# Per-tile norm factors, transposed halves of dt and one power for the last rows in a gMLP and Mamba-2 block on one core

## The chip, the cores and the metric

The kernel runs on one core of a Trainium2 chip. The metric is the device time of one execution in microseconds. Five engines work side by side, each through its own list of instructions in order: PE (TensorE, products and transposes), DVE (VectorE), ACT (ScalarE), POOL (GpSimd) and SP (SyncE, which issues most loads). ACT issues the stores. The profile shows each instruction with its source line, its tiles, and what ended the idle time ahead of it.

## The reference

One layer on a sequence of 1024 rows and 1024 columns, all in float32: an adaptive norm whose scale and shift come from a conditioning vector, one wide projection, a gated spatial branch, a state-space branch, two projections back, and a final norm. What the change touches:

```python
def rms_norm(x, w):
    xf = x.astype(jnp.float32)
    y = xf * lax.rsqrt(jnp.mean(xf * xf, axis=-1, keepdims=True) + EPS)
    return (y * w.astype(jnp.float32)).astype(x.dtype)

mod = jax.nn.silu(c) @ ada_w + ada_b
shift, scale, gate = jnp.split(mod, 3, axis=-1)
h = rms_norm(x, norm_w) * (1 + scale[:, None, :]) + shift[:, None, :]
proj = h @ w_in
...
dt = jax.nn.softplus((dt_raw + dt_bias).astype(jnp.float32))
...
x = x + gate[:, None, :] * (merged @ w_out)
return rms_norm(x, final_norm_w)
```

The norm of `h` needs one factor for each row, the power -1/2 of its mean square; dt_raw is 32 columns of the projection; the last line needs such a factor again.

## The kernel before

**Products.** Each large product is done with seven half-size products of the Strassen-Winograd kind (p1 to p7), and each float32 operand is split into a high and a low part (`hi`, `lo`, names that end in h and l), so that a product is three passes over four 128x512 pieces (L591). A bank in PSUM is emptied by a copy or an addition (L728, results such as c1g, c2g, c2z, c2x: letters for columns group, numbers for the halves of rows). p4 of a group adds onto a bank that the addition into c2 must have read before, so PE waits for that VectorE instruction.

**Head.** Eight tiles of x (128 rows each, `xt`, x_238 to x_245 in the lists below) are loaded. `square` (L376, ACT) gives a tile's sums of squares, `factors` (L380 on VectorE, L381 on GpSimd) the factors of four tiles at once, `normed` scales half a tile (left columns are half 0). Then PE transposes pieces of the scaled tiles (L94, px), a matrix-vector product `matvec` (L91, pm<-aw,scz) and `modulation` give scale and shift (md), and `rows_of_h` writes the transposed h and its parts (hf, b11h, b11l; b12 for tiles 4 to 7). The first weights are split in `split_w0` (w0l, w0d). Products with ones and the identity (`warm`, acc<-ones,ident) fill PE between. All of the head is written with `pin`: its order on each engine is that of the code. After the first product passes the loop calls `prepare(1)`, which makes the second half.

**Middle.** Beside the projection run three sorts of side work, spread over the products by `later(n, f)`, which puts f behind n more products: the quarters of the second projection's weights (`wb_quarter` and what follows it, tiles wbr, wba, wbb, wbc, stored to wb_d), the gate's weights (`gated_weights`, tile wog, stored to wo_d), and dt. The projection has left dt as two halves of 32 rows (one for the high and one for the low part of the operands) in dt_d, 64 rows by 1024. `dt_part1` loads them (dtt), `dt_part1a` brings them into rows by chunk and adds the two halves: eight products with `fold`, two identity pieces on top of one another, into the bank pdtt, with the bias added as the bank is read (L806). Steps with the tile sm (L807 to L836) compute softplus from it. What is not pinned here is ordered on VectorE and ScalarE by a scheduler that works from its own costs, so one more instruction can move many others.

**Tail.** The last product leaves rows in banks; `after_bank` adds them to the rows' tile r, squares, takes the factor with one power on GpSimd (`roots_of`, L1958 and L1959) and scales (L2007, L2008). The last row tile is done in two pieces of 256 columns (L2049 to L2057); its factor is computed by `last_root`, three Newton steps on VectorE from an integer estimate (L1964 to L1968).

```python
    mm(pt[:, ch * NH : (ch + 1) * NH], dtt[:, ch * P : (ch + 1) * P], fold[0][0 : 2 * NH, :])
V.tensor_tensor(v3(dtr), v3(pt[:, 0:n]), bc(dtb), op=ALU.add)
...
last_root(3)
V.tensor_scalar_mul(rows[3][:, LEFT], rows[3][:, LEFT], root[:, 3:4])
```

Of the kernel before, what the change touches and what calls it, by code (L numbers as in the profile page):

```python
# [16 lines left out]
P = 128  # L17
# [6 lines left out]
NH = 32  # L24
# [11 lines left out]
def hybrid_kernel(  # L36
# [106 lines left out]

    hpool = tc.tile_pool(name="hpool", bufs=1, reuse_waits="tile")
    hp = hpool.__enter__()
    BANKS = (1, 2, 0, 4, 5, 6, 3, 7)
    BN = ("b11", "t1", "t2", "b22", "t3", "b21", "t4")
    bop = {}
    for nm in BN:
# [30 lines left out]
    with tc.tile_pool(name="p0", bufs=1, reuse_waits="tile") as p0:  # L180
# [72 lines left out]
        def warm(n):  # L253

            for _ in range(n):
                mm(accs[2][1][:, 0:P], ident, ones)
# [118 lines left out]
        def square(t):  # L375
            pin(A.activation(junk, xt[t], AF.Square, accum_out=sq0[:, t : t + 1]))  # L376

        def factors(b):
            bs = slice(4 * b, 4 * b + 4)
            pin(V.tensor_scalar(sq0[:, bs], sq0[:, bs], 1.0 / D, EPS, op0=ALU.mult, op1=ALU.add))  # L380
            pin(G.tensor_tensor(rs[:, bs], sq0[:, bs], nhalf[:, bs], op=ALU.pow))  # L381

# [6 lines left out]

        for t in range(4):  # L390
            square(t)
        factors(0)
        for t in range(4):
            normed(t, 0, V)
        transposes(0, 0)
        split_w0(0)
        for t in range(4):
            normed(t, 1, V)
        matvec(0)
        warm(3)  # L400
        modulation(0)
        warm(8)
        rows_of_h(0, 0)
        for t in range(4, NCH):
            square(t)
        factors(1)
        for half in range(2):
            for t in range(4, NCH):
                normed(t, half, A if t > 5 else V)
        split_w0(1)  # L410

        def prepare(n):

            if n == 1:
                return {
                    8: lambda: (warm(6), transposes(0, 1), rows_of_h(0, 1), matvec(1), warm(5)),
                    11: lambda: (transposes(1, 1), modulation(1), rows_of_h(1, 1)),
                    16: lambda: (transposes(1, 0), rows_of_h(1, 0)),
                }
            a, b = halves(n)  # L420
            return {
                2: lambda: (matvec(n), transposes(n, a)),
                6: lambda: (modulation(n), rows_of_h(n, a)),
                14: lambda: (transposes(n, b), rows_of_h(n, b)),
            }
# [360 lines left out]
    def dt_part1():  # L786

        dtt = wide("dtt2")[0 : 2 * NH, :]
        load(dtt, dt_d)
        load(dtb, dt_bias.to_broadcast([P, NH]))  # L790
        load(abc, a_log.to_broadcast([P, NH]))
        V.tensor_add(fold[0], ident[:, 0:NH], ident[:, NH : 2 * NH])
        sm1 = wide("sm1").rearrange("p (a n) -> p a n", a=4)
        sm2 = wide("sm2").rearrange("p (a n) -> p a n", a=4)
        later(2, dt_part1a, dtt, sm1, sm2)

    def dt_part1a(dtt, sm1, sm2):
        v3 = lambda t: t.rearrange("p (a b) -> p a b", a=NCH)
        bc = lambda t: t.unsqueeze(1).to_broadcast([P, NCH, NH])
        n = NCH * NH  # L800
        e, q, pl, dtr = (sm1[:, i] for i in range(4))
        dth, adt = sm2[:, 0], sm2[:, 1]
        pt = bank("pdtt")
        for ch in range(NCH):
            mm(pt[:, ch * NH : (ch + 1) * NH], dtt[:, ch * P : (ch + 1) * P], fold[0][0 : 2 * NH, :])
        V.tensor_tensor(v3(dtr), v3(pt[:, 0:n]), bc(dtb), op=ALU.add)  # L806
        V.scalar_tensor_tensor(e, dtr, -1.0, dtr, op0=ALU.mult, op1=ALU.max)  # L807
        A.activation(e, e, AF.Exp, scale=-1.0)
        later(2, dt_part1b, e, q, pl, dtr, dth, adt)
# [616 lines left out]
        return done  # L1426

    todo = jobs + tail
    fold = []
    NPRE = 19  # L1430
    pre = None
    ops = pair_weights(*todo[0][:3], pinned=True)
# [4 lines left out]
    for n, (name, _, _, d1, d2, g) in enumerate(todo):  # L1437
        if n == 3:
            later(1, mix_load, 0)
        if n == NPRE:  # L1440
            gate_kept()
            gxpool.__exit__(None, None, None)
            prepool = tc.tile_pool(name="prepool", bufs=1, side="right", reuse_waits="tile")
            pre = prepool.__enter__()

            fold.append(pre.tile([P, NH], F32, name="fold", tag="fold"))
            wb_load(0)
            for i in range(len(quarters)):
                later(2 + 4 * i, wb_quarter, i)
# [388 lines left out]
    ps3 = tc.tile_pool(name="ps3", bufs=1, space=PSUM, reuse_waits="tile")  # L1838
    psb = ps3.__enter__()
    numbered(psb, "q")  # L1840
    places_of = {"x": (3, 1, 0, 2), "y": range(4, 8)}
    assert all(b > 3 for b in free[6:])
    OB = {"p1": 0, "p5": 1, "p7": 2, "p4": 3, "p6": 4, "p2": 5, "p3": 6}
    OORDER = ("p1", "p5", "p6", "p7", "p4", "p3", "p2")
# [113 lines left out]
        V.scalar_tensor_tensor(var[:, ts], sql[:, ts], 1.0 / D, sqr[:, ts], op0=ALU.mult, op1=ALU.add)  # L1958
        G.tensor_tensor(root[:, ts], var[:, ts], nhalf[:, ts], op=ALU.pow)  # L1959

    def last_root(t):

        y, t, v = root[:, 3:4], sql[:, 4:5], sql[:, 5:6]
        V.tensor_scalar(y.bitcast(I32), var[:, 3:4].bitcast(I32), -0.5, float(0x5F3759DF), op0=ALU.mult, op1=ALU.add)  # L1964
        V.tensor_scalar_mul(v, var[:, 3:4], -0.5)
        for _ in range(3):
            V.scalar_tensor_tensor(t, y, y, v, op0=ALU.mult, op1=ALU.mult)
            V.scalar_tensor_tensor(y, t, 1.5, y, op0=ALU.add, op1=ALU.mult)  # L1968

    def multiplied(ps, nm, j, cs, w):  # L1970
        a, first = mop[OUT[nm][1]], nm in ("p1", "p5", "p2")
        for k in range(4):
# [67 lines left out]
    for nm in OORDER:  # L2040
        ps, m = out_banks[OUT[nm][0]], OUT[nm][1]
        if nm == "p2":
            variance(slice(0, 4))
        for j in range(4):
            if nm == "p2" and j == 3:
                pieces = ((ps[3][:, 0:256], slice(0, 256)), (banks_last[:, 0:256], slice(256, 512)))
                for n, (acc, cs) in enumerate(pieces):
                    multiplied(acc, nm, 3, cs, 256)
                    V.tensor_add(rows[3][:, cs], rows[3][:, cs], acc)  # L2049
                    square(3, cs, sql[:, 3 + 4 * n : 4 + 4 * n])  # L2050
                    G.tensor_mul(rows[3][:, cs], rows[3][:, cs], fnw[:, cs])
                    V.scalar_tensor_tensor((sqr if n == 0 else var)[:, 3:4], sql[:, 3 + 4 * n : 4 + 4 * n], 1.0 / D,
                                           sqr[:, 3:4], op0=ALU.mult, op1=ALU.add)
                last_root(3)
                V.tensor_scalar_mul(rows[3][:, LEFT], rows[3][:, LEFT], root[:, 3:4])
                out_leave(3, LEFT, nc.sync)
                A.mul(rows[3][:, RIGHT], rows[3][:, RIGHT], root[:, 3:4])  # L2057
                out_leave(3, RIGHT, nc.scalar)
                continue
            if nm == "p1":  # L2060
                row_tile(j)
                row_tile(4 + j)
                load(rows[4 + j], x[(4 + j) * P : (5 + j) * P, :])
            multiplied(ps[j], nm, j, slice(0, 512), 512)
            after_bank(nm, j, ps[j])
            beside_bank(nm, j)
        if nm != "p2":
            release_m(m)
            release_w(nm)
        if nm == "p4":  # L2070
            variance(slice(4, 8))
            roots_of(slice(4, 8))
            for t in range(4, 8):
                V.scalar_tensor_tensor(rows[t], rows[t], root[:, t : t + 1], fnw, op0=ALU.mult, op1=ALU.mult)
                out_leave(t, slice(0, D), nc.sync)
        if nm == "p3":
            banks_last = psb.tile([P, 512], F32, name="olast", tag=f"q{places_of['x'][0]}")
# [34 lines left out]
```

## Time and profile before

| what | value |
|---|---|
| three runs | 1381.2, 1381.89, 1385.27 us; median 1381.89 |
| profiled execution | 1381.81 us, of which the span is 1380.1 |
| mean granted TensorE clock | 0.998 |
| PE, DVE, ACT, POOL busy | 1360.0, 1058.1, 793.4, 200.1 us |
| first product of h / last product pass starts | 19.53 us / 1372.39 us |
| last output transfer issued by ACT | 1376.62 us |

A row of the timeline reads: start, duration, engine, line, operation, output<-inputs, partitions by elements and type, how many instructions, and in brackets the idle time ahead of it with what ended it. A row of the waits reads: engine, what waited, what it waited for, then total, count and longest in us. A row of the windows reads: from:to, length, then for PE, PE's weight loads, DVE, ACT and POOL the busy time with the number of instructions, then the granted clock, the busy share of the DMA engines, and GB/s.

### The profile page before, as it was taken

How to read it: one execution, taken by the hardware profiler on the slowest of the kernel's cores; microseconds unless marked ns; L12 is line 12 of the kernel's file. 1: busy time of each engine (PE TensorE's matmuls, PEld its weight loads, DVE VectorE, ACT ScalarE, POOL GpSimd, SP SyncE). 2: the span in 40 equal slices, each digit the busy share in tenths (PEclk: the TensorE clock that was granted, in tenths of full speed). 3: DMA queues.
4: the chain of work that ended last, by engine and by line, in shares of the span. 5: the costliest groups of instructions: out<-in, count | busy, mean ns of one | idle time of the engine just before them, and what ended most of it. 6: DMA issues, size and time to landing. Idle time of an engine off the chain costs nothing.

```text
span 1380.1 us, 20352 instructions
## 1 busy us (share of the span) xinstructions
PE 1360.0 (99%) x6955; PEld 1123.4 (81%) x6955; DVE 1058.1 (77%) x1792; ACT 793.4 (57%) x1466; POOL 200.1 (14%) x201
## 2 busy tenths in 40 slices
PE   8999999999999999999999999999999999999997
PEld 7788888888888887888877888888888878888886
DVE  5675766887777688779889987577888787778975
ACT  6764456666666656556556655576877744233543
POOL 0000000000000000000000000006898881000012
PEclk9999999999999999999999999999999999999999
DMA  9574533545423346687776885579989959977733
GB/s 279 164 247 148 171 91 112 170 124 160 122 80 104 122 140 178 191 241 227 241 245 209 250 255 170 168 255 320 323 277 323 298 169 280 395 277 283 260 116 122
DMA packets 272364, 286.58 MB, mean 208 GB/s; under 512 B 18780, under 2 KB 215812, under 8 KB 272260
## 3 DMA queue, kind: packets, MB, share of 16 engines
q1 hardware_dynamic: 196100, 214.35, 49.4%
q10 hardware_dynamic: 76160, 70.92, 15.0%
q8 instruction: 55, 0.90, 0.3%
q14 instruction: 49, 0.40, 0.1%
HBM read 198.77 MB, written 86.44 MB: 207 GB/s over the span
## 4 chain that ended last, share of the span: by engine, by line
PE 81%; DVE 7%; DMA 5%; issue 2%; ACT 2%; SPq 1%; POOL 1%; ACTq 0%; DVEq 0%; POOLq 0%
PE x L1722 6%; PE xuz L591 6%; PE xx L591 5%; PE xz L591 5%; PE pma L91 5%; PE xcb L591 5%; PE yp L1722 5%; PE xg L591 4%; PE ou L1974 3%; PE vx L703 3%; PE yuz L591 3%; PE yx L591 3%; PE ycb L591 2%; PE vy L703 2%; PE yz L591 2%
## 5 line engine op out<-in xcount | busy, mean ns | idle before, releaser
L56 POOL TENSOR_SCALAR_AFFINE_SELECT dcy<-dcy 128x1024 f32<-128x1024 f32 x32 | 35.0, 1093 | 784.5 <-DVE yh L56 738.2
L56 ACT ACTIVATE dcy<-dcy,nacs 128x128 f32<-128x128 f32 x256 | 78.7, 391 | 18.3 <-POOL dcy L56 18.0
L56 ACT ACTIVATE ea<-dcy 64x512 f32<-64x512 f32 x64 | 40.4, 632 | 7.5 <-DMA dcy<-acs_d 6.9
L91 PE MATMUL pma<-yh,wah 128*128 128x512 f32 x128 | 43.0, 417 | 0.0
L91 PE MATMUL pma<-yh,wal 128*128 128x512 f32 x128 | 42.6, 414 | 0.0
L56 POOL TENSOR_TENSOR yz<-y,sl 128x512 f32<-128x512 f32 x32 | 41.9, 1311 | 0.6
L1041 ACT ACTIVATE ac<-ac 128x1024 f32<-128x1024 f32 x32 | 34.0, 1063 | 12.9 <-DVE ac L1039 12.8
L56 DVE TENSOR_TENSOR ym<-yn,ea 128x512 f32<-128x512 f32 (+1 forms) x32 | 20.0, 624 | 27.4 <-PE yn L91 27.4
L56 DVE TENSOR_TENSOR dcy<-dcy,pc 128x1024 f32<-128x1024 f32 x32 | 38.9, 1217 | 2.1 <-PE pc L94 1.2
L91 PE MATMUL pma<-yl,wah 128*128 128x512 f32 x128 | 39.9, 393 | 0.0
L56 POOL TENSOR_TENSOR y<-y,ym 128x512 f32<-128x512 f32 (+1 forms) x32 | 38.5, 1203 | 8.8 <-DVE ym L56 8.6
L1039 DVE SCALAR_TENSOR_TENSOR ac<-c2cb,cwt,ac 128x1023 f32<-128x1023 f32 (+2 forms) x24 | 30.7, 1281 | 6.9 <-ACT ac L1037 6.8
L91 PE MATMUL yi<-dcy,xd 128*64 128x128 f32 x512 | 35.0, 279 | 0.3 <-DVE xd L56 0.3
L1039 DVE SCALAR_TENSOR_TENSOR ac<-c2x,cwt,ac 128x1023 f32<-128x1023 f32 (+2 forms) x24 | 30.7, 1280 | 5.8 <-ACT ac L1037 5.7
L91 PE MATMUL sp<-xe,bn 128*128 128x256 f32 x112 | 32.7, 409 | 0.0
L91 PEld LDWEIGHTS yi<-dcy,xd 128*64 128x64 f32 x512 | 27.3, 136 | 6.4 <-issue 4.1
L56 DVE SCALAR_TENSOR_TENSOR yn<-yn,par,rb 128x512 f32<-128x512 f32 x32 | 25.8, 806 | 7.9 <-DMA yn<-yb_d 7.8
L1039 DVE SCALAR_TENSOR_TENSOR ac<-c1x,cwt,ac 128x1023 f32<-128x1023 f32 (+2 forms) x24 | 30.8, 1282 | 0.7 <-ACT ac L1037 0.7
L1039 DVE SCALAR_TENSOR_TENSOR ac<-c1cb,cwt,ac 128x1023 f32<-128x1023 f32 (+2 forms) x24 | 30.8, 1283 | 0.0
L2035 POOL TENSOR_TENSOR r<-r,xr 128x512 f32<-128x512 f32 x4 | 6.3, 1582 | 168.9 <-ACT wohp L1856 167.9
L56 DVE SCALAR_TENSOR_TENSOR y<-sl,dskt,yi 128x256 f32<-128x256 f32 x64 | 27.6, 474 | 1.2 <-POOL yz L56 1.2
L1003 ACT ACTIVATE vm<-vm,vr 128x128 f32<-128x128 f32 x64 | 25.7, 489 | 4.8 <-DMA vm<-v_d 4.8
(2913 smaller groups left out, 4357.0 us busy)
## 6 DMA issues: line engine op xcount, KB each, us to landing
sl<-s_d SPq DMA_DIRECT2D x32, 768.0 KB
s_d<-ac ACTq DMA_DIRECT2D x32, 512.0 KB
dcy<-acs_d SPq DMA_DIRECT2D x32, 512.0 KB
aw<-in_ada_w_dram SPq DMA_DIRECT2D x16, 512.0 KB
vp<-in_w_in_dram SPq DMA_DIRECT2D x32, 256.0 KB
wbr<-in_w_proj_b_dram SPq DMA_DIRECT2D x64, 128.0 KB
wb_d<-wbb ACTq DMA_DIRECT2D x32, 256.0 KB
wb_d<-wbc ACTq DMA_DIRECT2D x32, 256.0 KB
```

Source lines behind the costliest of these rows:

```text
L56: return lambda *a, **k: tc.keep_in_program_order(f(*a, **k))
L91: pin(PE.matmul(acc, l, r, start=first, stop=last))
L591: pin(PE.matmul(ps, lw[:, k * P : (k + 1) * P], r[k], start=first and n + k == 0, stop=n == 2 and k == 3, skip_group_check=not first))
L703: pin(PE.matmul(ps[j], l[k][:, js], r, start=first and k + m == 0, stop=k == 3 and m == 2, skip_group_check=not first))
L1003: A.activation(vn[:, cs], vn[:, cs], AF.Identity, scale=vr[:, 1, ch : ch + 1], bias=vr[:, 2, ch : ch + 1])
L1039: V.scalar_tensor_tensor(ac[:, s:], cc[:, : S - s], conv_wt[:, 3 - s, i : i + 1], ac[:, s:], op0=ALU.mult, op1=ALU.add)
L1041: A.activation(ac, ac, AF.Silu)
L1722: pin(PE.matmul(ps[j], a[:, v, js], r, start=first and n + k == 0, stop=n == 2 and k == KT - 1, skip_group_check=not first))
L1974: pin(PE.matmul(ps, a[k][v][:, j * P : (j + 1) * P], wop[nm, k][r][:, cs], start=first and n + k == 0, stop=n == 2 and k == 3, skip_group_ ...
L2035: G.tensor_add(rows[j][:, LEFT], rows[j][:, LEFT], xr.pop(j))
```

## The change

- Head: `factors` takes one tile; each of tiles 0 to 3 is scaled (left half) as soon as its factor is there, and so are tiles 4 to 7, all on VectorE. `matvec(0)` stands ahead of `split_w0(0)`, so VectorE's row copy too. The right halves of tiles 0 to 3 come later: 0 and 1 among tiles 5 and 6, 2 and 3 on ScalarE. `split_w0(1)` moves into `prepare`, behind `matvec(1)`.
- dt: eight transposes in place of eight products; the bank's second half is copied by ScalarE, the two halves are added, then the bias. The tile `fold` and its one addition are gone.
- Tail: `last_root` is gone, one power on GpSimd takes its place. The product with the final weight goes to a tile of its own (`last`) and no longer over the rows that ScalarE still squares.
- The numbers of PSUM banks for seven operands and for four output banks are in another order.

```diff
-    BANKS = (1, 2, 0, 4, 5, 6, 3, 7)
+    BANKS = (1, 2, 0, 4, 3, 6, 5, 7)
...
-        def factors(b):
-            bs = slice(4 * b, 4 * b + 4)
+        def factors(t):
+            bs = slice(t, t + 1)
...
             square(t)
-        factors(0)
-        for t in range(4):
+            factors(t)
             normed(t, 0, V)
         transposes(0, 0)
+        matvec(0)
         split_w0(0)
-        for t in range(4):
-            normed(t, 1, V)
-        matvec(0)
         warm(3)
...
             square(t)
-        factors(1)
-        for half in range(2):
-            for t in range(4, NCH):
-                normed(t, half, A if t > 5 else V)
-        split_w0(1)
+            factors(t)
+            normed(t, 0, V)
+            if t in (5, 6):
+                normed(t - 5, 1, V)
+        for t in range(4, NCH):
+            normed(t, 1, V)
+        for t in (2, 3):
+            normed(t, 1, A)
...
-                    8: lambda: (warm(6), transposes(0, 1), rows_of_h(0, 1), matvec(1), warm(5)),
+                    8: lambda: (warm(6), transposes(0, 1), rows_of_h(0, 1), matvec(1), split_w0(1), warm(5)),
...
-            mm(pt[:, ch * NH : (ch + 1) * NH], dtt[:, ch * P : (ch + 1) * P], fold[0][0 : 2 * NH, :])
-        V.tensor_tensor(v3(dtr), v3(pt[:, 0:n]), bc(dtb), op=ALU.add)
+            tp(pt[:, 2 * ch * NH : 2 * (ch + 1) * NH], dtt[:, ch * P : (ch + 1) * P], ident[0 : 2 * NH, 0 : 2 * NH])
+        p4 = pt.rearrange("p (a v b) -> p v a b", a=NCH, v=2)
+        A.copy(v3(q), p4[:, 1])
+        V.tensor_tensor(v3(dtr), p4[:, 0], v3(q), op=ALU.add)
+        V.tensor_tensor(v3(dtr), v3(dtr), bc(dtb), op=ALU.add)
...
-    places_of = {"x": (3, 1, 0, 2), "y": range(4, 8)}
+    places_of = {"x": (1, 3, 0, 2), "y": range(4, 8)}
...
+                last = [t[:, 256 * n : 256 * n + 256] for t in (slot_tile("last"),) for n in range(2)]
...
-                    G.tensor_mul(rows[3][:, cs], rows[3][:, cs], fnw[:, cs])
+                    G.tensor_mul(last[n], rows[3][:, cs], fnw[:, cs])
...
-                last_root(3)
-                V.tensor_scalar_mul(rows[3][:, LEFT], rows[3][:, LEFT], root[:, 3:4])
+                G.tensor_tensor(root[:, 3:4], var[:, 3:4], nhalf[:, 3:4], op=ALU.pow)
+                for t, (acc, cs) in zip(last, pieces):
+                    V.tensor_scalar_mul(rows[3][:, cs], t, root[:, 3:4])
```

PE's and SP's orders stay as they were, but for the transposes. Three places in VectorE's order, by line, operation, output<-inputs and shape. The first is the head, behind the low part of the first h (b11l), before:

```order
L313 TENSOR_TENSOR b11l_168<-hf_248,b11h_164 128x512
L380 TENSOR_SCALAR sq_329<-sq_329 128x4
L388 TENSOR_SCALAR x_242<-x_242,rs 128x512
L388 TENSOR_SCALAR x_243<-x_243,rs 128x512
L388 TENSOR_SCALAR x_242<-x_242,rs 128x512
L388 TENSOR_SCALAR x_243<-x_243,rs 128x512
L234 TENSOR_TENSOR w0l_279<-w0r_276,w0h_278 128x256
```

and in the change:

```order
L313 TENSOR_TENSOR b11l_168<-hf_248,b11h_164 128x512
L380 TENSOR_SCALAR sq_329<-sq_329 128x1
L388 TENSOR_SCALAR x_242<-x_242,rs 128x512
L380 TENSOR_SCALAR sq_329<-sq_329 128x1
L388 TENSOR_SCALAR x_243<-x_243,rs 128x512
L388 TENSOR_SCALAR x_238<-x_238,rs 128x512
L380 TENSOR_SCALAR sq_329<-sq_329 128x1
L388 TENSOR_SCALAR x_244<-x_244,rs 128x512
L388 TENSOR_SCALAR x_239<-x_239,rs 128x512
L380 TENSOR_SCALAR sq_329<-sq_329 128x1
L388 TENSOR_SCALAR x_245<-x_245,rs 128x512
```

One step over four tiles has become four, each with a scaled left half behind it, and tiles 6 and 7 (x_244, x_245) have come from ScalarE; the right halves of tiles 0 and 1 (x_238, x_239) stand between.

The second place is near 692 to 697 us, where dt's steps (sm) meet the gate's weights (wog) and the quarters (wba, wbb, wbc, wbr). Before:

```order
L812 TENSOR_SCALAR sm_6176<-sm_6176 128x256
L813 RECIPROCAL sm_6176<-sm_6176 128x256
L933 TENSOR_TENSOR wog_6239<-wog_6239,gb 128x1024
L537 TENSOR_TENSOR p6cb6l<-s2cb_6191,p6cb6h 128x512
L969 TENSOR_TENSOR wbc_6500<-wbr_6295,wbc_6500 128x2x128
L814 TENSOR_TENSOR sm_6176<-sm_6176 128x256
L969 TENSOR_TENSOR wba_6553<-wbr_6383,wba_6553 128x128
L537 TENSOR_TENSOR p3cb6l<-s4cb_6192,p3cb6h 128x512
L938 TENSOR_TENSOR wog_6238<-wog_6239,wog_6238 128x512
```

and in the change, whose lines are two further down:

```order
L935 TENSOR_TENSOR wog_6249<-wog_6249,gb 128x1024
L537 TENSOR_TENSOR p6cb6l<-s2cb_6201,p6cb6h 128x512
L833 TENSOR_SCALAR sm_6186<-sm_6186 128x256
L971 TENSOR_TENSOR wbb_6510<-wbr_6307,wbb_6510 128x2x128
L989 TENSOR_TENSOR wbr_6307<-wbr_6307 128x128
L814 TENSOR_SCALAR sm_6186<-sm_6186 128x256
L940 TENSOR_TENSOR wog_6248<-wog_6249,wog_6248 128x512
L971 TENSOR_TENSOR wba_6565<-wbr_6395,wba_6565 128x128
L537 TENSOR_TENSOR p3cb6l<-s4cb_6202,p3cb6h 128x512
L815 RECIPROCAL sm_6186<-sm_6186 128x256
```

The product of wog with gb now stands ahead of the reciprocal (and of the step that waits for the exponential), not behind it. Further on, near 706 us, wbb and wba stand behind the addition into c2g and no longer ahead of it.

The third place is near 748 us, ahead of the addition into c2z that PE waits for. Before:

```order
L969 TENSOR_TENSOR wba_7048<-wbr_6884,wba_7048 128x128
L848 TENSOR_TENSOR dde<-dde,dthq 128x256
L581 TENSOR_TENSOR s2g_6812<-s1g_6811,a11g_6803 128x512
L583 TENSOR_TENSOR a21g_6805<-a11g_6803,a21g_6805 128x512
L537 TENSOR_TENSOR p4x6l<-a22x_6592,p4x6h 128x512
L858 TENSOR_SCALAR act<-pact_6778 32x512
L728 TENSOR_TENSOR c2z_6801<-p5z_6668,xz_6631 128x512
```

and in the change:

```order
L580 TENSOR_TENSOR s1g_6823<-a21g_6817,a22g_6819 128x512
L940 TENSOR_TENSOR wog_6694<-wog_6695,wog_6694 128x512
L537 TENSOR_TENSOR p4x6l<-a22x_6604,p4x6h 128x512
L860 TENSOR_SCALAR act<-pact_6790 32x512
L728 TENSOR_TENSOR c2z_6813<-p5z_6680,xz_6643 128x512
L971 TENSOR_TENSOR wba_7060<-wbr_6896,wba_7060 128x128
L860 TENSOR_SCALAR act<-pact_6796 32x512
L581 TENSOR_TENSOR s2g_6824<-s1g_6823,a11g_6815 128x512
L583 TENSOR_TENSOR a21g_6817<-a11g_6815,a21g_6817 128x512
```

s2g, a21g and wba have moved from ahead of c2z to behind it.

More of the change, by code (lines that the diff above doesn't have):

```diff
@@ L791, in dt_part1 @@
         load(abc, a_log.to_broadcast([P, NH]))
-        V.tensor_add(fold[0], ident[:, 0:NH], ident[:, NH : 2 * NH])
         sm1 = wide("sm1").rearrange("p (a n) -> p a n", a=4)
@@ L1428, in hybrid_kernel @@
     todo = jobs + tail
-    fold = []
     NPRE = 19
@@ L1444, in hybrid_kernel @@
             pre = prepool.__enter__()
-            fold.append(pre.tile([P, NH], F32, name="fold", tag="fold"))
             wb_load(0)
@@ L1959, in roots_of @@
         G.tensor_tensor(root[:, ts], var[:, ts], nhalf[:, ts], op=ALU.pow)
[L1961 to L1968, printed above, removed]
     def multiplied(ps, nm, j, cs, w):
```

## The prediction

> **What bounds the kernel now.** I read the page's busy shares and chain first, then PE's waits behind the start-up, then the timeline around each long wait.
>
> ```profile
> PE 1360.0 (99%) x6955; PEld 1123.4 (81%) x6955; DVE 1058.1 (77%) x1792; ACT 793.4 (57%) x1466; POOL 200.1 (14%) x201
> PE 81%; DVE 7%; DMA 5%; issue 2%; ACT 2%; SPq 1%; POOL 1%; ACTq 0%; DVEq 0%; POOLq 0%
> PE xz L591 <- DVE c2z L728: 2.7, 1, 2.7
> PE xg L591 <- DVE c2g L728: 2.3, 1, 2.3
> ```
>
> PE is busy for 99% of the span and makes 81% of the chain that ended last. From 26 to 1375 us it waits five microseconds for two VectorE additions, and for nothing else that long. So the time can only move in three places: ahead of the first long stretch of products (to 26 us), at these two waits, and behind the last product. The change touches all three. An edit elsewhere costs nothing while PE has work: the same stretch that holds both waits has slack on VectorE as a mean (65 of 76 us), so the waits are a matter of order, not of load.
>
> ```profile
> 684.00:760.00 76.00, 70.99 (x316) 57.82 (x315) 65.03 (x135) 43.97 (x75) 0.00 (x0) 0.98 0.73 227
> ```
>
> **The middle: dt.** Removed on PE are eight fp32 products with the folded identity, added eight transposes.
>
> ```profile
> 684.46 1.97 PE L91 MATMUL pdtt<-fold,dtt 64*128 64x32 f32 x16
> 686.36 1.19 PE L591 MATMUL xz<-t4h,p4z3h 128*128 128x512 f32 x4
> 741.69 1.04 PE L94 MATMUL pact<-ident,nacs 128*32 128x128 f32 x8
> 742.49 1.18 PE L591 MATMUL xx<-b11h,p1x6h 128*128 128x512 f32 x4
> ```
>
> The 16 passes held PE for 686.36 - 684.46 = 1.90 us. Eight transposes with 32 columns held it for 742.49 - 741.69 = 0.80. The new ones have 64: 0.80 if columns count for nothing, 1.6 if twice of them take twice as long; I take 1.2 between, as the trace shows none, a gain of 0.7 (0.3 to 1.1). The ScalarE copy and the second addition (256 elements each, 0.4 us like the 128x256 rows below) are not waited for by PE for tens of us; what they do is to push the small steps behind them, and with them the computed order of VectorE and ScalarE up to 900 us. That decides more than the instructions themselves. The two waits:
>
> ```profile
> 692.60 1.75 DVE L813 RECIPROCAL sm<-sm 128x256 f32<-128x256 f32 x1
> 693.56 1.28 ACT L1047 ACT_TABLE_LOAD   x1
> 702.55 0.69 DVE L942 TENSOR_TENSOR wog<-wog,wog 128x512 f32<-128x512 f32 x1 [1.70 <-DMA wo_d<-wog]
> 706.10 0.42 DVE L969 TENSOR_TENSOR wbb<-wbr,wbb 128x256 fp32r<-128x256 f32 x1
> 707.98 1.21 PE L591 MATMUL xg<-t4h,p4g8h 128*128 128x512 f32 x4 [2.26 <-DVE c2g L728]
> ```
>
> First wait, 2.26 us: c2g comes late because VectorE, which works in order, stood 1.70 at L942 until an earlier store had left wog's tile, with c2g behind. The gated product (L933) that this store waits for stands behind the reciprocal of 1.75 now, and ahead of it in the new order: the store leaves early enough, and the 1.70 goes. wbb (0.42) and wba (half as wide, 0.2) move behind c2g, with their starts 0.34 and 0.2 apart: 0.55. Against it: the exponential comes later in ScalarE's queue, and its two table loads (1.28 each, as above) now stand ahead of the casts of wba and p3cb6, whose VectorE halves wait in order: about 1.15 of that is not covered. So 2.26 - 1.70 - 0.55 + 1.15 = 1.2 us are left. From below nothing is left, if the table loads find VectorE busy; from above 2.9, if the store is no earlier and 1.70 stays.
>
> ```profile
> 716.45 0.41 ACT L964 CAST wbc<-wbr 128x256 fp32r<-128x256 f32 x1 [1.91 <-DMA wb_d<-wbc]
> 716.88 0.43 DVE L969 TENSOR_TENSOR wbc<-wbr,wbc 128x256 fp32r<-128x256 f32 x1 [2.06 <-ACT wbc L964]
> 747.85 0.69 DVE L581 TENSOR_TENSOR s2g<-s1g,a11g 128x512 f32<-128x512 f32 x1
> 748.45 0.69 DVE L583 TENSOR_TENSOR a21g<-a11g,a21g 128x512 f32<-128x512 f32 x1
> 750.25 0.66 DVE L728 TENSOR_TENSOR c2z<-p5z,xz 128x512 f32<-128x512 f32 x1
> 750.97 1.24 PE L591 MATMUL xz<-t4h,p4z4h 128*128 128x512 f32 x4 [2.75 <-DVE c2z L728]
> ```
>
> Second wait, 2.75 us: VectorE stood 2.06 for a ScalarE cast that itself stood 1.91 for a store, and never made that up until c2z. In the new order that cast stands two 128x512 steps later on ScalarE and its VectorE half four steps later on VectorE, so the store has up to 1.9 us more; and s2g and a21g (0.60 each by their starts) and wba (0.2), 1.4 together, stand behind c2z. 2.06 and 1.4 are more than 2.75; I leave 0.4 for what the first wait hands on.
>
> The second wait costs more than its length: the clock falls behind it.
>
> ```profile
> 748.57:751.98 3.41, 1.01 (x4) 0.86 (x5) 3.41 (x6) 2.80 (x4) 0.00 (x0) 1.00 0.42 129
> 751.98:755.39 3.41, 3.41 (x9) 2.63 (x8) 2.58 (x7) 2.31 (x5) 0.00 (x0) 0.50 1.02 352
> 704.19:707.61 3.42, 1.53 (x7) 0.94 (x5) 3.42 (x9) 2.29 (x4) 0.00 (x0) 1.00 0.37 144
> ```
>
> The stretch of 3.41 us that holds the wait had PE busy for 1.01; the next ran at a granted clock of 0.50, with PE busy throughout: half of 3.41, 1.7 us, is lost. The first wait left 1.53 busy in its stretch, and the clock stayed at 1.00. So with the second wait its 1.7 goes as well.
>
> The sum of the middle: -(2.26 + 2.75 + 1.7) = -6.7; +1.2 and +0.4 left over; -0.7 of dt. PE now arrives some 5 us earlier at the same VectorE work, so I look at what is late next:
>
> ```profile
> 767.88 0.68 DVE L728 TENSOR_TENSOR c2x<-p5x,xx 128x512 f32<-128x512 f32 x1
> 771.77 1.07 PE L591 MATMUL xx<-t4h,p4x6h 128*128 128x512 f32 x4
> 786.11 0.68 DVE L728 TENSOR_TENSOR c2g<-p5g,xg 128x512 f32<-128x512 f32 x1
> 790.81 1.07 PE L591 MATMUL xg<-t4h,p4g10h 128*128 128x512 f32 x4
> ```
>
> c2x is done at 768.56, 3.2 us ahead of its product; the next c2g at 786.79, 4.0 ahead. PE takes that away, while VectorE gains its own waits too (2.06 + 1.70 of standing idle, in part): if it came forward not at all, c2x would be 4.9 - 3.2 = 1.7 late, and 2.4 with one step of 0.69 put ahead of it; if as far as PE, nothing. I put 0.8, half of the 1.7. **Middle: -6.7 + 1.6 + 0.8 - 0.7 = -5.0 us**, between -7.8 and -1.3 with all bounds at one end.
>
> **The head.** Up to b11l it becomes earlier:
>
> ```profile
> 14.81 1.07 PE L91 MATMUL pm<-aw,scz 128*32 128x256 f32 x16
> 15.09 1.67 DVE L388 TENSOR_SCALAR x<-x,rs 128x512 f32<-128x512 f32 x4
> 16.67 0.42 DVE L275 COPY row<-pm 128x256 f32<-128x256 f32 x1
> 19.42 0.69 DVE L313 TENSOR_TENSOR b11l<-hf,b11h 128x512 fp32r<-128x512 f32 x1
> 20.69 1.02 POOL L381 TENSOR_TENSOR rs<-sq,nhalf 128x4 f32<-128x4 f32 x1 [7.90 <-DVE sq L380]
> 21.46 1.50 PE L91 MATMUL acc<-ones,ident 128*128 128x128 f32 x12
> 23.58 1.07 PE L91 MATMUL pm<-aw,scz 128*32 128x256 f32 x16
> 26.11 0.73 PE L91 MATMUL acc<-b,w0h 128*128 128x512 f32 x2
> ```
>
> The row copy stood behind four right halves until 16.67, though its products ended at 15.88: 0.8; a tile's factor right behind its squares lets the transposes begin some 0.35 sooner. So b11l starts near 18.3 and VectorE is free near 18.9. But now four tiles go through VectorE, GpSimd and VectorE again, in order, and each VectorE step waits: sq to factor to scaled tile. The price of such a round is read in the tail, where 1371.99 to 1372.80 is one (below): 0.82, and 0.41 for the scaled half (1.67 / 4), 1.23 a tile. With two right halves between (0.82): 18.9 + 4.9 + 0.8 = 24.6 for the last scaled tile, 24.8 for matvec(1), whose distance to the next long stretch stays 26.11 - 23.58 = 2.5: 27.3 instead of 26.11, **+1.2 us**. From below: rounds as short as 0.65 (the smaller pow without its hand-overs) give +0.4; from above, GpSimd's 1.02 of the 128x4 row gives +1.4 once a tile's square hides a part. The casts of the second weights, moved behind matvec(1), have that 2.5 as cover.
>
> **The tail.**
>
> ```profile
> 1371.99 0.16 DVE L1958 SCALAR_TENSOR_TENSOR dthq<-dthq 128x1 f32<-128x1 f32 x1 [0.30 <-ACT junk L1938]
> 1372.23 0.54 POOL L1959 TENSOR_TENSOR dthq<-dthq,nhalf 128x1 f32<-128x1 f32 x1 [2.47 <-DVE dthq L1958]
> 1372.80 0.72 ACT L2008 ACTIVATE r<-r,dthq 128x512 f32<-128x512 f32 x1 [0.30 <-POOL dthq L1959]
> 1373.96 0.16 DVE L2052 SCALAR_TENSOR_TENSOR dthq<-dthq 128x1 f32<-128x1 f32 x1
> 1375.86 0.72 ACT L2057 ACTIVATE r<-r,dthq 128x512 f32<-128x512 f32 x1 [1.94 <-DVE dthq L1968]
> ```
>
> From the last variance to ScalarE's multiplication now 1.90 us, eight VectorE steps; by one pow as in the row above 0.81. Against it: GpSimd's first product into the new tile no longer waits for ScalarE's square, starts near 1371.7 and holds the pow of row 2 by 0.3; ScalarE's next steps, and the last variance, come 0.3 later. 1.09 - 0.3 = **-0.75 us** (-0.4, if the hold is the 0.7 of a whole GpSimd product; -1.1 without it). VectorE's own half, in two pieces, still ends ahead of ScalarE's 0.72.
>
> The bank numbers change which earlier reader a product waits for; the one wait among these that PE shows is 0.4 us on an unchanged reader. Nothing.
>
> **Sum**, against the profiled execution's 1381.81 (span 1380.1, 1.7 outside; the median of the runs shown is 1381.89): +1.2 - 5.0 - 0.75 = -4.55, **1377.3 us**.
>
> **Where a rule and a row differ.** In the new head the warm-up products (12 passes, to 22.96 now) end 1.1 us sooner, near 21.8, and two transposes later, from about 22.1, PE has one transpose until the last one at 24.7: gaps of 1.0 and 1.5 us. The Trainium skill, "TensorE: Matmul & The Clock Gate", Part 1: The HAM clock gate, has the clock halve after one idle window of about 3.4 us, free-running; gaps of 2.5 would not reach it. This trace differs from it: a wait of 2.75 was enough (1.01 busy). By the rule the sum stays 1377.3; by the trace it may grow by 1.7.
>
> **The rivals.** (A) The head's gap halves the clock. Of 3.41 us with the whole gap inside, 0.9 is busy, under the 1.01 that did it. The stretches of this trace, counted back from 748.57 in the 13 steps of 3.414 that lie down to 704.19, have one from 21.4 to 24.8, over the gap; but nothing shows that their phase repeats, and placed at random they hold the gap in one case of four. Price 1.7: 1379.0.
> (B) The first wait stays at its bound of 2.9, as the store leaves no earlier and the casts behind the table loads hold VectorE as well. Being over 2.75 it halves the clock too, and PE then comes no earlier to what follows: -6.7 + 2.9 + 1.7 + 0.4 - 0.7 = -2.4 instead of -5.0, 1379.9. For it speaks that ScalarE feeds three of VectorE's steps there; against, that L933 stands ahead of the reciprocal in the new order.
> (C) Slower: the reordered stores of wb and wog hold VectorE once more ahead of c2x or c2g, so that the two old waits stay and a third of 2.75 with its half clock (4.45) comes: +1.2 - 0.75 - 0.7 + 4.45 = +4.2, 1386.0. It decides once c2x ends 3.2 + 2.75 = 6 us later against PE than now; the slack and ScalarE's 44 of 76 us speak against it, the stands of 1.70 and 1.91 for such stores for it.
> (D) The waits go wholly (neither 1.6 nor 0.8 is left): 1374.9; with the head at its lower bound 1374.1.
>
> **Chances.** Forecast 0.42, alone 1375.5 to 1378.6; A 0.22; B 0.12; C 0.14; D 0.10. About 0.3% (4.1 us) is what a measurement can tell from no change: faster means under 1377.7. That takes two thirds of the forecast, a fifth of A, all of D and some spread below: 0.50. Slower, over 1386.0, takes half of C and what lies beyond, 0.15. The rest, 0.35, is the same. The range, 1374.3 to 1384.5, leaves out the end of D and most of C.
>
> **What would show it.** b11l near 18.3, and acc products on b12 near 27.3; the granted clock in 25 to 28.5 (A). Eight transposes in 1.2 us. PE's waits for c2g near 707 and c2z near 750: 1.2 and 0.4, and clock 1.00 behind the second. New waits at the xx and xg products 20 and 40 us later (B, C). The last multiplication of ScalarE 0.8 us behind the last variance. If PE's waits between 680 and 900 sum to over 6 us, the middle of this prediction is wrong.

## The result, and the profile after

| | before | change |
|---|---|---|
| median of ten runs | 1382.19 us | 1378.53 us (1375.56 to 1380.99) |
| ratio | | 0.9968, 95% interval 0.9957 to 0.9979 |
| profiled execution, span | 1381.81, 1380.1 us | 1379.03, 1377.3 us |

The ratio is 4.4 us of 1382 (2.9 to 5.9). It is "the same" by a bound of 2%, and at the edge of the 0.3% that the prediction took for it. 4.55 had been forecast.

The page of the changed kernel, busy time by engine and then the chain that ended last, shows as little as before: PE still sets the time.

```profile
PE 1358.4 (99%) x6947; PEld 1121.2 (81%) x6947; DVE 1058.2 (77%) x1793; ACT 788.0 (57%) x1465; POOL 203.1 (15%) x208
PE 80%; DVE 6%; DMA 6%; issue 3%; POOL 2%; ACT 1%; SPq 0%; ACTq 0%; POOLq 0%; DVEq 0%
```

To see where the time went I set each of PE's instructions beside the same one of the execution before, and took the difference of their starts in the two profiled executions:

| first products behind | before | change | difference |
|---|---|---|---|
| b11 parts (head) | 19.53 | 18.09 | -1.44 |
| matvec(1) | 23.58 | 24.72 | +1.14 |
| b12 parts (head's end) | 26.11 | 28.33 | +2.22 |
| dt's eight instructions begin | 684.46 | 686.47 | +2.01 |
| next product | 686.36 | 687.11 | +0.75 |
| p4 of xg (first wait) | 707.98 | 708.70 | +0.72 |
| p4 of xz (second wait) | 750.97 | 749.08 | -1.89 |
| p6 of xx (behind the half clock) | 755.42 | 751.93 | -3.49 |
| p4 of xg, later one | 790.81 | 788.18 | -2.63 |
| last product | 1372.39 | 1370.17 | -2.22 |
| ScalarE's last multiplication | 1375.86 | 1372.98 | -2.88 |

So in this pair of executions the head costs 2.2 us, the middle gains 4.6 up to 790 us, another 0.4 is lost behind that in the state-space stage, and the tail gains 0.66.

**Head.** The timeline of PE and that of VectorE in the changed kernel, with start, duration, and in brackets the idle time ahead:

```profile
18.09 0.70 PE L91 MATMUL acc<-b11h,w0h 128*128 128x512 f32 x2
...
22.77 0.33 PE L94 MATMUL px<-ident,x 128*128 128x128 f32 x1 [1.01 <-DVE x L388]
24.37 0.41 PE L94 MATMUL px<-ident,x 128*128 128x128 f32 x1 [1.28 <-DVE x L388]
24.72 1.93 PE L91 MATMUL pm<-aw,scz 128*32 128x256 f32 x16
26.58 1.99 PE L91 MATMUL acc<-ones,ident 128*128 128x128 f32 x10
28.33 0.71 PE L91 MATMUL acc<-b,w0h 128*128 128x512 f32 x2
```

```profile
17.98 0.69 DVE L313 TENSOR_TENSOR b11l<-hf,b11h 128x512 fp32r<-128x512 f32 x1
18.59 0.15 DVE L380 TENSOR_SCALAR sq<-sq 128x1 f32<-128x1 f32 x1
19.40 0.49 DVE L388 TENSOR_SCALAR x<-x,rs 128x512 f32<-128x512 f32 x1 [0.66 <-POOL rs L381]
...
23.83 2.07 DVE L388 TENSOR_SCALAR x<-x,rs 128x512 f32<-128x512 f32 x5 [0.66 <-POOL rs L381]
```

A round takes 19.40 - 18.59 = 0.81 to the scaled half, of which VectorE stands still for 0.66. matvec(1) starts at 24.72 and then takes 1.93 where it took 1.07: the clock. The windows of the same execution, cut within 0.1 us of where it fell (the third figure from the right is PE's granted clock; PE's busy time is the first behind the length):

```profile
20.99:24.40 3.41, 1.12 (x9) 0.69 (x8) 2.08 (x8) 1.37 (x4) 1.10 (x2) 1.00 0.82 223
24.40:27.81 3.41, 3.41 (x23) 1.93 (x23) 3.09 (x8) 2.50 (x6) 0.00 (x0) 0.51 0.84 244
```

1.12 us of work in 3.41, then 3.41 us at half clock.

**Middle.** PE in the changed kernel, and then the three VectorE rows that matter ahead of the first wait:

```profile
686.47 0.71 PE L94 MATMUL pdtt<-ident,dtt 64*128 64x64 f32 x8
687.11 1.21 PE L591 MATMUL xz<-t4h,p4z3h 128*128 128x512 f32 x4
...
699.24 1.19 PE L591 MATMUL xg<-t3h,p7g8h 128*128 128x512 f32 x4 [0.92 <-ACT c1g L728]
...
708.70 1.20 PE L591 MATMUL xg<-t4h,p4g8h 128*128 128x512 f32 x4 [1.00 <-DVE c2g L728]
749.08 1.20 PE L591 MATMUL xz<-t4h,p4z4h 128*128 128x512 f32 x4 [0.20 <-DVE c2z L728]
788.18 1.21 PE L591 MATMUL xg<-t4h,p4g10h 128*128 128x512 f32 x4 [0.73 <-DVE c2g L728]
```

```profile
698.22 0.29 DVE L971 TENSOR_TENSOR wba<-wbr,wba 128x128 fp32r<-128x128 f32 x1 [1.43 <-ACT wba L966]
...
699.35 1.75 DVE L815 RECIPROCAL sm<-sm 128x256 f32<-128x256 f32 x1
...
702.08 0.69 DVE L944 TENSOR_TENSOR wog<-wog,wog 128x512 f32<-128x512 f32 x1
```

The op of the 1.70 wait (L944 now) waits for nothing, and the wait that ScalarE's table loads cause is there, 1.43. ScalarE's own copy of a bank (c1g) comes late by them too: a wait of 0.92 at a place where PE had none.

**Tail.** All engines, in order of time:

```profile
1369.61 0.73 POOL L2042 TENSOR_TENSOR last<-r,fnw 128x256 f32<-128x256 f32 x1 [2.09 <-DVE r L2040]
...
1369.76 0.60 DVE L1957 SCALAR_TENSOR_TENSOR dthq<-dthq 128x1 f32<-128x1 f32 x1 [0.29 <-ACT junk L1937]
...
1370.44 0.54 POOL L1958 TENSOR_TENSOR dthq<-dthq,nhalf 128x1 f32<-128x1 f32 x1
...
1372.40 0.54 POOL L2045 TENSOR_TENSOR dthq<-dthq,nhalf 128x1 f32<-128x1 f32 x1 [0.70 <-DVE dthq L2043]
1372.98 0.72 ACT L2049 ACTIVATE r<-r,dthq 128x512 f32<-128x512 f32 x1 [0.85 <-POOL dthq L2045]
```

From the last product's start to ScalarE's last multiplication it was 1375.86 - 1372.39 = 3.47 and is 1372.98 - 1370.17 = 2.81.

### The profile page after: what moved, and what is told of

The parts are those of the page before. It is cut to its first block, busy times and chain, and to the rows that moved or that the text cites. A ratio compares the mean times of both kernels' runs of the same rounds, so it can differ in the third digit from the quotient of the medians.

```text
span 1377.3 us, 20335 instructions
## 1 busy us (share of the span) xinstructions
PE 1358.4 (99%) x6947; PEld 1121.2 (81%) x6947; DVE 1058.2 (77%) x1793; ACT 788.0 (57%) x1465; POOL 203.1 (15%) x208
## 4 chain that ended last, share of the span: by engine, by line
PE 80%; DVE 6%; DMA 6%; issue 3%; POOL 2%; ACT 1%; SPq 0%; ACTq 0%; POOLq 0%; DVEq 0%
PE x L1721 6%; PE xuz L591 6%; PE xcb L591 5%; PE xx L591 5%; PE yp L1721 5%; PE pma L91 4%; PE xz L591 4%; PE xg L591 4%; PE ou L1964 3%; PE yuz L591 3%; PE vx L703 3%; PE acc L91 3%; PE ycb L591 3%; PE vy L703 2%; PE yx L591 2%
## 5 line engine op out<-in xcount | busy, mean ns | idle before, releaser
L91 PEld LDWEIGHTS pma<-yl,wah 128*128 128x128 f32 x128 | 24.0, 188 | 5.4
```

Of the source, the lines that this page charges most:

```text
L91: pin(PE.matmul(acc, l, r, start=first, stop=last))
```

## The experiments

Three comparisons on three chips, with medians of the kernel before of 1381.04, 1381.24 and 1380.83 us. Gains are worked out from the ratios.

### One part at a time

`e1_head`, `e2_dt` and `e3_tail` are the kernel before with one part of the diff above each, `e4_nohead` is the change without the head's part.

> Only the head's part of the change, on the kernel before. Theory (the four rounds between VectorE and GpSimd set the start of the products on b12, and the gap they leave halves the clock behind it): products on b12 at 28.3 us as in the change, 26.11 before, of which 1.2 us are rounds and 1.0 clock; time 2.0 to 2.4 us over the kernel before in the profile. Rival (the rounds cost, the clock's fall was a chance of one execution): 27.3 us and +1.2. Rival (the head is made up for in the middle, where PE then waits less): products late, the time within 0.5 us of the kernel before.

> Only dt's part (transposes, ScalarE copy, two additions, no fold tile), on the kernel before. Theory (the middle's gain is dt's alone, 1.3 us of it on PE and the rest by the order of VectorE and ScalarE): PE comes 4.2 to 4.6 us earlier to the products behind 900 us, time 4.2 us under the kernel before. Rival (the order gains only because PE arrives 2 us later from the head): the wait of xg for c2g near 707 us grows by some 1 to 2 us, and the gain is 2.5 us or less.

> Only the tail's part (one power on GpSimd in place of eight VectorE steps, the product with the weight into its own tile), on the kernel before. Theory: from the end of the last product to ScalarE's last multiplication 2.8 us instead of 3.5, time 0.7 us under the kernel before. Rival (the hold of row 2's factor takes it all): no difference.

> The change without its head's part (dt, tail and bank numbers as in the change). Theory: the head's cost of 2.2 us goes, products on b12 at 26.1, time 5.0 us under the kernel before, near 1377.2, and 1.5 to 2.2 under the change. Rival (PE, 2.2 us earlier, meets the same VectorE work and waits for it near 700 us): the same time as the change, 1378.5, with 2 us more of waits for c1g and c2g.

| kernel | median | ratio (95%) | us against before | head's end | last product |
|---|---|---|---|---|---|
| e1_head | 1382.62 | 1.0013 (1.0003 to 1.0023) | +1.8 | 28.56 | 1373.18 |
| e2_dt | 1376.37 | 0.9965 (0.9951 to 0.9978) | -4.8 | 27.41 | 1366.39 |
| e3_tail | 1380.44 | 0.9995 (0.9985 to 1.0005) | -0.7, not told from zero | 27.43 | 1371.03 |
| e4_nohead | 1375.36 | 0.9957 (0.9945 to 0.9970) | -5.9 | 25.93 | 1364.77 |

The parts do what the table of starts says: the head alone makes it slower, dt carries the gain, the tail is too small for the timed runs and shows in the trace alone (1373.85 - 1371.03 = 2.82). Without the head's part the change is 1.5 us better by the ratios, though the two intervals overlap.

The head's clock fell in `e1_head` as well; its windows:

```profile
21.42:24.83 3.41, 1.12 (x7) 0.59 (x6) 2.10 (x7) 1.51 (x4) 1.08 (x2) 1.00 0.65 185
24.83:28.24 3.41, 3.41 (x24) 2.13 (x24) 3.06 (x9) 2.71 (x6) 0.00 (x0) 0.50 0.92 267
```

But at the last product its profile is only 0.8 us behind (1373.18 against 1372.39), not 2.45. PE's waits and the clock say where the rest went. The first wait is as long as before, and here the clock falls behind it, at 711 us; PE then comes later to the second wait, which is 1.7 us shorter, and the half clock at 752 us does not come.

```profile
PE xg L591 <- DVE c2g L728: 2.2, 1, 2.2
PE xz L591 <- DVE c2z L728: 1.1, 1, 1.1
707.48:710.89 3.41, 1.24 (x6) 0.83 (x5) 3.41 (x9) 1.95 (x4) 0.00 (x0) 1.00 0.69 247
710.89:714.30 3.41, 3.41 (x9) 2.67 (x9) 3.41 (x11) 2.76 (x7) 0.00 (x0) 0.50 0.92 282
```

So in this one profile the third theory for `e1_head` holds in part. The timed runs do not bear it out: 1.8 us slower (0.4 to 3.2) is as much as the changed head costs on average (1.7, below). Nor is it shown that the head costs more in the new middle: the profiles of `e4_nohead` and of the change differ by 2.4 us at the head's end (25.93, 28.33) and by 5.4 at the last product (1364.77, 1370.17), but the ratios only by 1.5. The three parts sum to +1.8 - 4.8 - 0.7 = -3.7 us, and the change was measured at -4.4 and, again, at -3.3: within their intervals, of 1.3 to 1.9 us either way, the parts add.

One thing in the base was not as I had taken it. The unchanged head ended at 26.11 in the execution that I predicted from, but at 27.41 and 27.43 in two of these. ScalarE's rows of `e2_dt` have the reason: the last tile of x came later, 20.57 instead of 19.25.

```profile
20.57 1.06 ACT L376 ACTIVATE junk<-x 128x1024 f32<-128x1024 f32 x1 [1.71 <-DMA x<-in_x_dram]
```

With one factor for four tiles all four wait for it: in all seven profiled executions with the old head, the head ends 6.84 to 6.86 us behind the start of that row. In the changed head VectorE gets to the last tile's step at 23.02 only, so it does not notice. The seven end at 26.88 on average, the three with the changed head (28.33, 28.56, 28.87) at 28.59: the head costs 1.7 us by that, not 2.2.

### The change again

> The change as it is, on the chip of this comparison. Theory: ratio 0.997 to the kernel before as in the first comparison, and the clock falls in the head again (products on b12 at 28.3 us). Rival (the fall in the head was peculiar to the executions seen): products on b12 near 27.2 us, ratio near 0.995, as with the added warm-up products.

1377.89 us, ratio 0.9976 (0.9967 to 0.9986), 3.3 us: a little less than the first time, with overlapping intervals. The head's end is at 28.87, and the clock fell at another moment:

```profile
22.44:25.85 3.41, 1.14 (x14) 0.66 (x18) 2.30 (x7) 0.57 (x2) 0.96 (x2) 0.99 0.78 222
25.85:29.26 3.41, 3.41 (x23) 2.60 (x16) 3.02 (x7) 2.26 (x6) 0.00 (x0) 0.51 0.83 244
```

It fell in all three profiled executions with this head, each time behind 3.41 us with 1.12 to 1.14 busy, and there was no fall in the head of any profiled execution with another head.

### Filling the gap, and closing it

`e5_fill` gives PE something to do while it waits, on the whole change:

```diff
             for i in range(4):
+                if (n, h) == (0, 1) and i > 1:
+                    warm(4)
                 tp(px[:, i * P : (i + 1) * P], ...)
```

> The change, with four warm-up products ahead of each of the last two transposes of the second half's first piece, where PE waits in the head. Theory (the gap in PE's work halves the clock): granted clock 1.00 behind it, matvec(1) and the warm-up products behind it take 1.9 + 0.6 us instead of 3.6, products on b12 at 27.3 instead of 28.3 us, and the time 1 us under the change, 5.4 under the kernel before. Rival (the clock falls for another reason, or the added products delay the transposes): products on b12 at 28.3 or later, 4.4 under the kernel before or less.

```profile
24.59 0.33 PE L94 MATMUL px<-ident,x 128*128 128x128 f32 x1 [0.39 <-DVE x L390]
24.85 1.07 PE L91 MATMUL pm<-aw,scz 128*32 128x256 f32 x16
25.85 1.38 PE L91 MATMUL acc<-ones,ident 128*128 128x128 f32 x10
26.99 0.71 PE L91 MATMUL acc<-b,w0h 128*128 128x512 f32 x2
```

The last transpose is as late as in the change (24.59, 24.37 there), but matvec(1) takes 1.07 again and the head ends at 26.99, 1.3 and 1.9 us sooner than in the two executions of the change. The clock was the gap's doing: in this execution no stretch of 3.41 us in the head has less than 2.9 us of PE's work, wherever it begins. 1374.2 us, ratio 0.9947 (0.9934 to 0.9959), 7.3 us under the kernel before, where 5.4 was expected. The head explains 1.3 to 1.9 of the 3 to 4 us against the change; 0.7 more is the wait at 788 us, which this profile does not have; where the rest comes from was not taken apart.

`e6_pipe` keeps a factor for each tile, and lets the rounds overlap:

```diff
             square(t)
-            factors(t)
-            normed(t, 0, V)
-            if t in (5, 6):
-                normed(t - 5, 1, V)
+            if t < 7:
+                factors(t)
+        for t in range(4, 7):
+            normed(t, 0, V)
+        factors(7)
+        for t in (0, 1):
+            normed(t, 1, V)
+        normed(7, 0, V)
         for t in range(4, NCH):
             normed(t, 1, V)
```

> The change, with the rounds of tiles 4 to 7 laid over one another: VectorE's three steps for tiles 4, 5 and 6 come first, then their scaled halves, then tile 7's step, the right halves of tiles 0 and 1 while GpSimd works on it, and tile 7's scaled half. Theory (it is the waiting in each round that costs, not the number of factors): last scaled tile near 22.7 us instead of 24.3, products on b12 near 26.0, clock 1.00, time 2 us under the change, 6.4 under the kernel before. Rival (GpSimd's four calls cost by themselves): products on b12 at 27 us or later.

PE's row of the last transpose, and the end of the head:

```profile
23.29 0.33 PE L94 MATMUL px<-ident,x 128*128 128x128 f32 x1 [0.61 <-DVE x L388]
...
25.86 0.71 PE L91 MATMUL acc<-b,w0h 128*128 128x512 f32 x2
```

The head ends at 25.86, as early as the earliest execution of the old one (25.93 in `e4_nohead`), with four GpSimd calls as in the change: the waiting in each round was the cost, not the calls. The last tile was late here (its row at 20.33), and the head ends 5.53 us behind that, where the old one ended 6.84 behind it. 1375.09 us, ratio 0.9953 (0.9940 to 0.9965), 6.5 us.

### dt: the transposes or the order

Any edit of dt makes the scheduler compute another order, so the two can't be had wholly apart. `e7_dtorder` keeps the products with fold and adds as many steps as the change has; `e9_tponly` has the transposes and no step more than before; it leaves the second half of dt out of the sum.

```diff
+        A.copy(v3(q), v3(pt[:, 0:n]))
+        V.tensor_tensor(v3(dtr), v3(pt[:, 0:n]), v3(q), op=ALU.max)
-        V.tensor_tensor(v3(dtr), v3(pt[:, 0:n]), bc(dtb), op=ALU.add)
+        V.tensor_tensor(v3(dtr), v3(dtr), bc(dtb), op=ALU.add)
```

> The kernel before, with its eight products with fold kept, and after them the change's number of steps: a ScalarE copy of the sum, a maximum of the sum and its copy, the bias added. Its computed order has wog's product ahead of the reciprocal and s2g, a21g behind c2z, as the change has, though it is not the change's order row by row. Theory (the order carries most of the gain, PE's 1.3 us the rest): the two waits of 2.3 and 2.7 us shrink to 1 and 0.3, no half clock behind the second, time 3 us under the kernel before. Rival (the gain is the transposes' and what follows from PE): both waits as before, time within 1 us of the kernel before.

```diff
+            tp(pt[:, 2 * ch * NH : 2 * (ch + 1) * NH], dtt[:, ch * P : (ch + 1) * P], ident[0 : 2 * NH, 0 : 2 * NH])
+        p4 = pt.rearrange("p (a v b) -> p v a b", a=NCH, v=2)
+        V.tensor_tensor(v3(dtr), p4[:, 0], bc(dtb), op=ALU.add)
```

> The kernel before with the transposes, but without the ScalarE copy and the second addition: the second half of dt is left out of the sum, so there is no step more than before on ScalarE or VectorE. Its computed order is a fourth one, again with wog's product ahead of the reciprocal and s2g, a21g behind c2z. Theory: eight transposes in 0.65 us instead of 1.9, the two waits at 1 and 0.3 us, time 4 to 5 us under the kernel before, as with dt's whole part. Rival (the copy and the addition are needed for the order that gains): 1.3 us under the kernel before, both waits as they were.

In `e7_dtorder` PE's time for dt is the old one, and its two long waits are gone all the same; two of 0.9 for ScalarE's copies stand in their place:

```profile
686.06 1.97 PE L91 MATMUL pdtt<-fold,dtt 64*128 64x32 f32 x16
687.96 1.19 PE L591 MATMUL xz<-t4h,p4z3h 128*128 128x512 f32 x4
```

```profile
PE xx L591 <- ACT c1x L728: 0.9, 1, 0.9
PE xg L591 <- ACT c1g L728: 0.9, 1, 0.9
```

1377.21 us, ratio 0.9968 (0.9956 to 0.9980): 4.4 us gained without one transpose. `e9_tponly`, the transposes in the 0.64 us that they took in the change too, has no wait of PE over 0.6 before the state-space stage at all: 1374.44 us, ratio 0.9949 (0.9936 to 0.9961), 7.0 us. The order can carry the gain without a transpose. On PE the transposes take 1.3 us less than the products; the remainder between 4.4 and 7.0 lies in two different orders and was not taken apart. The copy and the addition that the change puts behind the transposes were not needed for an order that gains (4.8 in `e2_dt` against 7.0, with intervals that overlap).

### The bank numbers

`e8_banks`, the two lines of the diff alone.

> Only the numbers of the PSUM banks, on the kernel before. Theory: no wait of PE changes by more than 0.3 us but for the spread of executions, time within 0.5 us of the kernel before. Rival (a part of the gain is from banks read earlier): up to 1 us under the kernel before, with the wait of xcb for c2cb near 532 us gone.

1381.33 us, ratio 1.0004 (0.9995 to 1.0013). The wait of xcb near 532 us was not there in this profile, as the rival says, but with the whole change it was 0.4 and 0.8, so it comes and goes from one execution to the next, and the time shows nothing.

### What holds row 2's factor in the tail

`e10_tail2` is `e6_pipe` with one VectorE step in place of two GpSimd products and two VectorE ones:

```diff
-                    G.tensor_mul(last[n], rows[3][:, cs], fnw[:, cs])
...
-                for t, (acc, cs) in zip(last, pieces):
-                    V.tensor_scalar_mul(rows[3][:, cs], t, root[:, 3:4])
+                V.scalar_tensor_tensor(rows[3][:, LEFT], rows[3][:, LEFT], root[:, 3:4], fnw[:, LEFT],
+                                       op0=ALU.mult, op1=ALU.mult)
```

> The change with the overlapped rounds in the head (as in the second comparison), and a tail without GpSimd's two products with the final weight: VectorE multiplies the last rows' left half by factor and weight in one step, as it does for the other row tiles. Theory (a GpSimd product with two inputs holds a VectorE step with two inputs until it ends, so that the factor of row 2 and all behind it come 0.45 us late): VectorE's step ahead of row 2's power takes 0.16 instead of 0.60, ScalarE's last multiplication starts 2.35 instead of 2.8 us behind the end of the last product's start, and the time is 0.4 us under that with the overlapped rounds alone, 6.8 under the kernel before. Rival (VectorE's step is late because of ScalarE's accumulated sum): 0.60 again, and no gain.

```profile
1365.39 0.16 DVE L1961 SCALAR_TENSOR_TENSOR dthq<-dthq 128x1 f32<-128x1 f32 x1 [0.29 <-ACT junk L1941]
1365.63 0.54 POOL L1962 TENSOR_TENSOR dthq<-dthq,nhalf 128x1 f32<-128x1 f32 x1 [2.47 <-DVE dthq L1961]
...
1368.17 0.72 ACT L2051 ACTIVATE r<-r,dthq 128x512 f32<-128x512 f32 x1 [0.85 <-POOL dthq L2047]
```

0.16 instead of 0.60, and 1368.17 - 1365.80 (the last product's start here) = 2.37 instead of 2.81. 1374.25 us, ratio 0.9956 (0.9943 to 0.9970), 6.1 us: faster than before; under the change, which runs at 1377.89 in the same comparison, though the two intervals just overlap; and not to be told from `e6_pipe`. The 0.44 us of this step is shown by the traces alone.

## Why the prediction was right, point by point

- **The sum.** 1377.3 was forecast and 1378.53 measured, -4.55 against -4.4 by the ratio, in the range, by the mechanisms that were named, but for the head's half clock, which was named as a rival only. The two profiled executions differ by 2.8 and the medians by 3.7, so the ratio's 4.4 is the generous one of three figures, and that the sum met it so closely owes something to luck: the head and the first wait came out dearer, the transposes cheaper.
- **Head, +1.2.** The mechanism was right: b11's products 1.4 us sooner, rounds of 0.81 for the 0.82 that was taken from the tail, matvec(1) at 24.72 where 24.8 was forecast. The size was not: 2.2 in the profile, 1.7 by the averages above. The step that failed is the chance of rival A, 0.22. The clock fell in three of three, and `e5_fill` took that away. The argument was that a stretch of fixed length at any phase holds the whole gap in one case of four. But it need not hold the whole gap: stretches with up to 1.27 us of PE's work were followed by a fall (last section), and in the change's trace each stretch that begins between 20.82 and 21.90 has no more than that, which is a third of all placements. The price of 1.7 was an upper one; 1.1 to 1.6 was paid (28.33 - 24.72 = 3.6 us and its like from matvec(1) to the head's end, against 2.5 before and 2.1 in `e5_fill`).
- **The base of the head.** 26.11 was an early execution. Of the six others with the old head two ended at 25.93 and 26.42 (`e4_nohead`, `e8_banks`) and four at 26.99 to 27.87, when the last tile of x came late. Against the latest of these, 27.87, the change's 28.33 costs half a microsecond, against the average 1.5. One profiled execution does not tell how late a load can be, and this had no term.
- **dt on PE, -0.7.** Mis-sized: 1.90 became 0.64 us, 1.26 gained, beyond its own bound of 1.1. Eight with 64 columns and 64 rows took less than the 0.80 of the eight with 32 columns and 128 rows that it was read from.
- **First wait, 1.2 left.** The mechanism came as worked out: the 1.70 for the store is gone, the casts behind the table loads hold VectorE (1.43 for the 1.15). Left are 1.00 for c2g and, not foreseen, 0.92 at another product, for a bank that ScalarE copies: the table loads were followed to VectorE, but not to ScalarE's other work.
- **Second wait and half clock, 0.4 left.** Right: 0.20, and 1.6 us of clock back.
- **New waits, 0.8.** Right in size, 0.73, at the later c2g; c2x was in time.
- **Middle, -5.0.** -4.6 in the profile, -4.8 for dt's part alone (`e2_dt`). That an order alone can bring as much is shown by `e7_dtorder`, with an order that is not the change's row by row.
- **Tail, -0.75.** 0.66 in the trace. The hold of 0.3 was put down to GpSimd's queue; it is VectorE's step that was held, 0.44 us, as `e10_tail2` shows.
- **Rivals B and C.** Not seen in the change. B's price, a half clock behind the first wait, came in `e1_head`: a wait of 2.2 left 1.24 us of work in its stretch and the clock fell, where one of 2.3 had left 1.53 and it had not. The same wait can fall on either side, by where the stretch begins.
- **Slips in the working.** 1.09 - 0.3 is 0.79, not 0.75. The 4.9 by which PE was to come earlier to c2x has no sum behind it; 6.7 - 1.6 + 0.7 - 1.2 gives 4.6. Of the 0.50 for faster the named shares give 0.42, and of the 0.15 for slower half of C gives 0.07; the remainders were put down to spread without a figure. None of these moves the forecast by more than 0.2 us.

## What to carry to other kernels

Where a scheduler computes the order, an edit off the critical path is a new draw of the order on two engines: compare the listed orders ahead of the instructions that the bottleneck waits for, since more can lie there than in the edit's own cost (4.4 us by the order without a transpose, 1.3 on PE by the transposes). Splitting a batched step into rounds between two engines paid here only when the rounds overlapped: issue the first engine's steps for several tiles before the first result is used. And where the bottleneck engine has to wait and its clock falls for it, cheap work in the gap can keep the clock up: here that was worth 1.1 to 1.6 us on the way to the head's end.

## What the hardware showed that was not expected

**The clock.** Up to the last product, each fall of the granted clock in these traces came behind a stretch of 3.41 us in which PE worked for about a third: 1.01 us before, 1.12, 1.12 and 1.14 in the changed head, 1.24 in `e1_head` at 707 us, 1.27 in `e3_tail` and 1.09 in `e8_banks` at the second wait. Each was followed by 3.41 us at a granted clock near 0.5; stretches with 1.53 (before), 1.90 (`e10_tail2`) and 1.96 (`e3_tail`) were not. The limit lies between 1.27 and 1.53 here. The Trainium skill, "TensorE: Matmul & The Clock Gate", Part 1: The HAM clock gate, has the fall after an idle window; here no window was idle, a third busy was too little.

The falls lie on a fixed count: in each trace they are a whole number of 3.413 us behind the first record of the clock, five in the changed head (from 7.42 to 24.48, from 7.74 to 24.81, from 8.74 to 25.81), 218 in the kernel before (from 7.87 to 751.98). That first record comes between 6.65 and 9.43 us in the thirteen executions, so the count begins at another moment each time. In the change's trace a stretch placed at random would leave no more than 1.27 us in a third of the cases, and less than 1.53 in nearly half. By that, three falls in three executions are a matter of 3 to 9 chances in a hundred; whether something places the stretch over the gap stays open.

**GpSimd and VectorE.** A VectorE step with two inputs of 128x1 took 0.60 us and ended at 1370.36, where a GpSimd product of 128x256 ended at 1370.34; it took 0.16 without it. The Trainium skill, "SBUF — State Buffer", SBUF: two separate sides, has a pair of ports that a VectorE instruction with two SBUF inputs and a GpSimd one hold against each other for the whole instruction. The trace agrees.
